# GpSimd's arithmetic moved to VectorE, into copies' scale, and into six merged operations

## The chip, the cores and the metric

The kernel runs on one core of one Trainium2 chip. The metric is the device time of one execution in microseconds (us). A core has five engines with queues of their own: PE (TensorE, matrix products), DVE (VectorE), ACT (ScalarE), POOL (GpSimd) and SP (SyncE, which here only issues DMAs). Each engine works through its queue in order; an instruction that waits holds back all that is queued behind it on the same engine.

## What is computed

Two small transformer stacks run one after the other on 512 tokens of width 1024, in float32. The first has two layers of a mixer (pooling, differential attention and a bidirectional recurrent branch, gated and summed) with a feed-forward part; every sum is followed by a layer norm. The second has two layers with a sparse and a banded attention, whose queries and keys get a root-mean-square norm per head, a weight per head column, and on one branch a partial rotation:

```python
x = layer_norm(alpha * x + mix, ln1_g[l], ln1_b[l])
hid = jnp.square(jax.nn.relu(x @ w_up[l]))
x = layer_norm(alpha * x + hid @ w_down[l], ln2_g[l], ln2_b[l])
...
qa = partial_rope(rms_norm(qa.reshape(b, s_len, 8, 64), qn_a[l]), cos, sin)   # first 16 of 64 columns rotate
ka = partial_rope(rms_norm(ka.reshape(b, s_len, 1, 64), kn_a[l]), cos, sin)[:, :, 0]
qi = partial_rope(qi.reshape(b, s_len, 8, 64), cos, sin)
ki = partial_rope(ki.reshape(b, s_len, 1, 64), cos, sin)[:, :, 0]
qb = rms_norm(qb.reshape(b, s_len, 8, 64), qn_b[l])
kb = rms_norm(kb.reshape(b, s_len, 8, 64), kn_b[l])
```

## The kernel before

**Matrix products.** Every large product is made three times with float32 values split in two parts, high and low (`mm3`, L235 to L237): high by high, high by low, low by high. A weight chunk of 128x1024 arrives by an SP DMA into `wraw` (three buffers), ACT copies it to `whi` (L228, two buffers), and DVE subtracts to get `wlo` (L229, two buffers). PE then spends 24 matmuls on the chunk. So DVE has one subtraction in each chunk that PE must have before the third matmul of the chunk, and the next chunk's DMA needs a `wraw` that this subtraction has let go.

**The iterator beside.** `chunk` calls `next(self.beside, None)` once for each weight chunk; other work (in the feed-forward part of the first stack, the `ada` product of the second stack's modulation, L1274) is spread over chunks in that way. Which instruction goes where in an engine's queue is settled when the program is built, by the framework's estimate of when its inputs are there, not by the order of the source alone.

**The residual.** A layer-normed tile is written to DRAM without its weight and bias, and read back for the residual by `load_x`: two row vectors `lng` and `lnb` broadcast to 128 partitions, four tiles of 128x1024, and for each tile a product (L381) and a sum (L382) on GpSimd. It is called four times: in each layer of the first stack ahead of the `w_out` product (tiles `xr`, wanted by its first evacuation, L1141), and ahead of the feed-forward part (tiles `xo`, wanted by the first evacuation of `w_down`, L973). The place of the first call is the end of the recurrent branch: there DVE works on the last head pair's norm (L927 to L936, with an inverse root made of a dozen operations on 128x8, L304 to L321), PE on the branch product `merge1` (PSUM tile `mr`), and after it DVE merges the branches (`mgg`, L522, L523) for the `w_out` product.

**The second stack's heads.** `projections` makes `qi`, `qa`, `qb`, `kb` (128 x 4 x 512 each) and two small ones, `ki` and `ka`, one after another, with a norm (`head_norm`), a rotation (`rope`) and transposes (`z_split`, `z_T`) between the products. The norm's last step, the product with the head weight `gn`, is on GpSimd (L1323), and so are all 24 operations of a rotation (L1333 to L1335, four times six). The index scores (`ix`, L1447) and the top-k search (MAX8 L1461, MATCH_REPLACE8 L1462) run on DVE in the same stretch.

Of the kernel before, what the change touches and what calls it, by code (L numbers as in the profile page):

```python
# [10 lines left out]
F32 = mybir.dt.float32  # L11
F32R = mybir.dt.float32r
I32 = mybir.dt.int32
AF = mybir.ActivationFunctionType
# [122 lines left out]
def bcast(ap, n=128):  # L137
    return bass.AP(tensor=ap.tensor, offset=ap.offset, ap=[[0, n]] + [list(x) for x in ap.ap])
# [29 lines left out]
class Kern:  # L168
# [206 lines left out]
    def load_x(self, wk, x, xd, rows):  # L375

        nc = self.nc
        g, b = self.ln_rows(wk, rows)
        for tk in range(4):
            nc.sync.dma_start(x[tk], xd[:, tk, :])  # L380
            nc.gpsimd.tensor_tensor(out=x[tk], in0=x[tk], in1=g, op=OP.mult)  # L381
            nc.gpsimd.tensor_tensor(out=x[tk], in0=x[tk], in1=b, op=OP.add)  # L382


    def bias_setup(self, wk, pp):
# [626 lines left out]
    def layer1(self, l, xd, act, start):  # L1012
# [3 lines left out]
        with tc.tile_pool(name="mx", bufs=1) as mx:  # L1016
# [64 lines left out]
            with tc.tile_pool(name="rw", bufs=1) as rw:  # L1081
                wk = _Slots(rw, MERGE_SLOTS)

                def z_tile(p):
                    vv = wk.tile([128, 640], F32, name="rw_v")
                    nc.vector.memset(vv[:, 0:64], 0.0)
                    nc.vector.memset(vv[:, 576:640], 0.0)
                    rkv = (wk.tile([128, S], F32, name="rw_r"), wk.tile([128, S], F32, name="rw_k"), vv)
                    for i in range(3):
                        dst = vv[:, 64:576] if i == 2 else rkv[i]  # L1090
                        self.lin_fm(pp, w_in, 2048 + i * 512 + p * 128, 1, act, 8,
                                    lambda _, ps: self.shift(wk, ps, vec, i * 4 + p, None, dst))
# [12 lines left out]

                gates = self.gate_steps(mx, pp, act, w_in, hbg, pd, md, gd)
                done = [0]

                def fill(n):
                    for _ in range(n):  # L1110
                        next(gates, None)
                    done[0] += n

                fill.upto = lambda n: fill(max(n - done[0], 0))
                mg = []
                merge = self.merge1(wk, pp, yc, a["w_branch"][l, 2], md, gd, mg)

                def behind():
                    list(gates)
                    for p in range(2):  # L1120
                        t = wk.tile([128, S], F32, name="ycr")
                        nc.scalar.dma_start(t, yd[p])
                        yc[p] = yhl(p)
                        self.split(*yc[p], t)
                    next(merge)

                self.rwkv(wk, pp, l, vec, hb, ka, low, z_tile, y_out, fill, behind)
                for p in range(4):
                    self.dump(f"yc{l}{p}", yc[p])
                act = self.xT()  # L1130
                xd1 = self.dr.tile([128, 4, D], F32, name="xspill", bufs=2)
                next(merge)
                xr = [wk.tile([128, D], F32, name="xr") for _ in range(4)]
                self.load_x(wk, xr, xd, (0, 1) if l == 0 else (6, 8))
                cols = self.ln_cols(wk, (2 + l, 4 + l))
                st = self.new_stats(wk)
                for ch in range(2):
                    cs = slice(ch * 512, (ch + 1) * 512)

                    def ev(tk, ps):  # L1140
                        nc.vector.scalar_tensor_tensor(out=xr[tk][:, cs], in0=xr[tk][:, cs], scalar=alpha, in1=ps,  # L1141
                                                       op0=OP.mult, op1=OP.add)
                        self.stats(st[:, tk], xr[tk], ch)
                        if ch == 1:
                            self.norm_tile(wk, pp, xr[tk], st[:, tk], cols, tk, act, xd1, FILL["lag"][1])

                    self.lin_tm(pp, a["w_out"][l], [(ch * 512, (ch + 1) * 512)], mg, 8, ev,
                                own=wk, tail=FILL["tails"][1] if ch else 1)
# [5 lines left out]
            self.second_consts()  # L1154
        with tc.tile_pool(name="f1", bufs=1) as wk:
            xo = wk.tile([128, 4, D], F32, name="xo")
            self.load_x(wk, [xo[:, tk, :] for tk in range(4)], xd1, (2 + l, 4 + l))
            cols = self.ln_cols(wk, (6 + l, 8 + l))
            g2, b2 = self.ln_rows(wk, (6 + l, 8 + l), nc.gpsimd) if last else (None, None)
            st = self.new_stats(wk)  # L1160
# [24 lines left out]
                else:  # L1185
                    self.norm_tile(wk, pp, xo[:, tk, :], st[:, tk], cols, tk, box[0], xd2, FILL["lag"][2])

            self.beside = chain([None] * 6, self.ada(wk, pp, l, "xhat" if last else "araw"))
            self.ffn1(wk, pp, l, act, xo, after)
            list(self.beside)  # L1190
        if last:
# [116 lines left out]
        self.lag(tk, lambda: self.affine_T(wk, pp, xn, tk, k2["g"][:, 8 * i:8 * i + 8],  # L1308
                                           k2["s"][:, 16 * i:16 * i + 8], act, bufs), lag)

    def head_norm(self, wk, z, g, n):

        nc = self.nc
        ss = wk.tile([128, 4, n], F32, name="hss", bufs=2)
        for t in range(4):
# [4 lines left out]
        zz = z.rearrange("p t h d -> p (t h) d")  # L1320
        nc.vector.tensor_tensor(out=zz, in0=zz, in1=ss.rearrange("p t h -> p (t h)")[:, :, None]
                                .to_broadcast([128, 4 * n, 64]), op=OP.mult)
        nc.gpsimd.tensor_tensor(out=zz, in0=zz, in1=g[:, None, :].to_broadcast([128, 4 * n, 64]), op=OP.mult)  # L1323

    def rope(self, wk, z, n):
        nc = self.nc
        t = wk.tile([128, 4, n, 4, 8], F32, name="ropet", bufs=1)
        for tk in range(4):
            c = self.cos[:, tk, None, :].to_broadcast([128, n, 8])
            s = self.sin[:, tk, None, :].to_broadcast([128, n, 8])  # L1330
            x1, x2 = z[:, tk, :, 0:8], z[:, tk, :, 8:16]
            for i, (x, w) in enumerate(((x1, c), (x2, s), (x2, c), (x1, s))):
                nc.gpsimd.tensor_tensor(out=t[:, tk, :, i, :], in0=x, in1=w, op=OP.mult)  # L1333
            nc.gpsimd.tensor_tensor(out=x1, in0=t[:, tk, :, 0, :], in1=t[:, tk, :, 1, :], op=OP.subtract)
            nc.gpsimd.tensor_tensor(out=x2, in0=t[:, tk, :, 2, :], in1=t[:, tk, :, 3, :], op=OP.add)  # L1335

    def z_split(self, pp, z, dst):

        nc = self.nc
        for j in range(4):  # L1340
            ps = pp.tile([128, 4, 128], F32, name="tr")
            for tk in range(4):
                nc.tensor.transpose(ps[:, tk, :], z[:, tk, j * 128:(j + 1) * 128], self.ident)
            self.stack(dst, ps.rearrange("p a b -> p (a b)"), 2 * j)

    def stack(self, dst, ps, j):

        nc = self.nc
        for m, r in enumerate(HALVES):
            nc.scalar.activation(dst[r, j + m, :], ps[r], AF.Copy)  # L1350
        for m, r in enumerate(HALVES):
            nc.vector.tensor_tensor(out=dst[HALVES[1 - m], j + m, :], in0=ps[r], in1=dst[r, j + m, :].bitcast(F32),
                                    op=OP.subtract)

    def z_T(self, pp, z, dst):

        nc = self.nc
        split = isinstance(dst, tuple)
        for j in range(1 if split else 4):
# [4 lines left out]
            if split:  # L1364
                self.split(*dst, flat)
            else:
                nc.scalar.activation(dst[:, j, :], flat, AF.Copy)

    def attend(self, wk, pp, heads, qb, done=None):

# [146 lines left out]
    def projections(self, wk, zp, pp, l, act, zt, after):  # L1517
        nc, a = self.nc, self.a
        w_in = a["w_in_2"][l]
        gn = wk.tile([128, 4, 64], F32, name="gn")  # L1520
        nc.sync.dma_start(gn.rearrange("p a d -> p (a d)"), bcast(a["qkn"][l].rearrange("a d -> (a d)")))
        for j in (0, 2):
            nc.vector.tensor_scalar(gn[:, j, :], gn[:, j, :], 0.125, None, op0=OP.mult)

        def proj(cols, dst):
            w = sum(c1 - c0 for c0, c1 in cols)
# [17 lines left out]
        nc.vector.tensor_copy(zt["va"], sml[:, :, 0:128][:, :, 64:128])  # L1544
        ka = wk.tile([128, 4, 1, 64], F32, name="ka")
        nc.vector.tensor_copy(ka[:, :, 0, :], sml[:, :, 0:64])
        self.head_norm(wk, ka, gn[:, 1, :], 1)
        self.rope(wk, ka, 1)
        dup = []
        for src in (ki, ka):  # L1550
            dd = wk.tile([128, 4, 2, 64], F32, name="dup", bufs=2)
            nc.gpsimd.tensor_copy(dd[:, :, 0, :], src[:, :, 0, :])
            nc.gpsimd.tensor_copy(dd[:, :, 1, :], src[:, :, 0, :])
            dup.append(dd.rearrange("p t a d -> p t (a d)"))
        qi = z()
        proj([(640, 1152)], qi)
# [6 lines left out]
        after()  # L1563
        qk = zp.tile([128, 8, S], F32, name="qkb", tag="qiT")
        zt["qbT"], zt["kbT"] = qk[:, :4], qk[:, 4:]
        self.head_norm(wk, hv(qa, 8), gn[:, 0, :], 8)
        self.rope(wk, hv(qa, 8), 8)
        qb = z()
        proj([(1224, 1736)], qb)
        self.z_split(pp, qa, zt["qaT"])  # L1570
        self.head_norm(wk, hv(qb, 8), gn[:, 2, :], 8)
        kb = z()
        proj([(1736, 2248)], kb)
        self.z_T(pp, qb, zt["qbT"])
        self.head_norm(wk, hv(kb, 8), gn[:, 3, :], 8)
        proj([(2248, 2760)], zt["vb"])
        self.z_T(pp, kb, zt["kbT"])

    def gate_steps2(self, wk, pp, act, w_in, hb, gd):

# [206 lines left out]
```

## Time and profile before

| | |
|---|---|
| median of 3 runs | 3813.1 us (3811.29 to 3816.84) |
| the profiled execution | 3811.36 us |
| its span, first to last instruction | 3809.4 us |
| PE busy | 3653.1 us, 96% of the span |
| DVE busy | 2272.0 us, 60% |
| ACT busy | 1381.6 us, 36% |
| POOL busy | 294.8 us, 8% |
| granted clock of TensorE, mean | 0.986 of full speed |

Busy time of DVE counts an instruction from its start to its end, and so also the time in which it stands still in the middle. A granted clock of 1.00 is 2.4 GHz, of 0.50 is 1.2 GHz.

### The profile page before, as it was taken

Reading aid. Unit: us, or ns where it says so; the run is one execution under the profiler, and the core shown is the slowest. Engines: PE = TensorE matmul, PEld = TensorE weight load, DVE = VectorE, ACT = ScalarE, POOL = GpSimd, SP = SyncE. Lnnn points to the kernel's source line nnn. Section 1 sums busy time; section 2 is a strip of 40 time slices with the busy share of each in tenths; the row PEclk is TensorE's granted clock in tenths of the full one; section 3 lists DMA queues with packets and bytes.
Section 4 is the critical chain, followed back from the end, with each engine's and each line's share of the span. In section 5 each row is a group of like instructions: output and inputs, shape, how many; then the busy total and the mean of one; then the engine's idle time right before and its main releaser. Section 6 shows DMA issues by size and latency. Waiting matters only on the chain. (4 is left out here: it accounts for less than half of the span.)

```text
span 3809.4 us, 54409 instructions
## 1 busy us (share of the span) xinstructions
PE 3653.1 (96%) x21264; PEld 2845.4 (75%) x21264; DVE 2272.0 (60%) x4679; ACT 1381.6 (36%) x2361; POOL 294.8 (8%) x445
## 2 busy tenths in 40 slices
PE   8999997999999999997899989999999999999999
PEld 6677775778877777765788776768888877678887
DVE  5667775765566577757655549866333369664333
ACT  4543332332334443332323234454222343534221
POOL 0000002110000000002300032000000041000000
PEclk9999999999999999998999999999999999999999
DMA  4333332555552333234555532334332323253332
GB/s 147 122 106 94 84 93 99 169 162 183 165 159 83 101 101 84 79 101 134 169 182 172 163 108 67 114 106 158 99 95 98 116 89 89 78 172 121 97 97 94
DMA packets 509392, 452.22 MB, mean 119 GB/s; under 512 B 87984, under 2 KB 405104, under 8 KB 509136
## 3 DMA queue, kind: packets, MB, share of 16 engines
q1 hardware_dynamic: 492032, 400.88, 34.5%
q0 software_dynamic: 10192, 32.15, 2.4%
q10 hardware_dynamic: 6912, 15.73, 1.2%
q8 instruction: 167, 2.74, 0.3%
q14 instruction: 89, 0.73, 0.1%
HBM read 395.68 MB, written 53.01 MB: 118 GB/s over the span
## 5 line engine op out<-in xcount | busy, mean ns | idle before, releaser
L229 DVE TENSOR_TENSOR wlo<-wraw,whi 128x1024 fp32r<-128x1024 f32 (+2 forms) x496 | 624.9, 1260 | 817.2 <-ACT whi L228 802.0
L228 ACT ACTIVATE whi<-wraw 128x1024 fp32r<-128x1024 f32 (+2 forms) x496 | 523.3, 1055 | 1520.6 <-PE acc L236 612.3
L235 PE MATMUL acc<-xTh,whi 128*128 128x512 f32 (+1 forms) x2320 | 917.7, 396 | 4.5 <-ACT whi L228 2.1
L237 PE MATMUL acc<-xTh,wlo 128*128 128x512 f32 (+1 forms) x2320 | 901.8, 389 | 19.1 <-DVE wlo L229 19.1
L236 PE MATMUL acc<-xTl,whi 128*128 128x512 f32 (+1 forms) x2320 | 899.7, 388 | 3.8 <-POOL xTl L359 1.8
L237 PEld LDWEIGHTS acc<-xTh,wlo 128*128 128x128 f32 x2320 | 438.9, 189 | 109.8 <-DVE wlo L229 20.8
L235 PEld LDWEIGHTS acc<-xTh,whi 128*128 128x128 f32 x2320 | 438.3, 189 | 109.8 <-issue 19.4
L236 PEld LDWEIGHTS acc<-xTl,whi 128*128 128x128 f32 x2320 | 439.2, 189 | 88.5 <-issue 5.1
L235 PE MATMUL tm<-whi,hidh 128*128 128x512 f32 x784 | 307.2, 392 | 0.9 <-DVE xo L975 0.8
L236 PE MATMUL tm<-wlo,hidh 128*128 128x512 f32 x784 | 306.5, 391 | 0.0
L237 PE MATMUL tm<-whi,hidl 128*128 128x512 f32 x784 | 306.5, 391 | 0.0
L235 PEld LDWEIGHTS tm<-whi,hidh 128*128 128x128 f32 x784 | 147.2, 188 | 35.6 <-issue 3.2
L235 PE MATMUL tm<-whi,xTh 128*128 128x512 f32 (+1 forms) x448 | 171.0, 382 | 1.6 <-DVE zt L1532 1.6
L237 PEld LDWEIGHTS tm<-whi,hidl 128*128 128x128 f32 x784 | 147.2, 188 | 31.9
L236 PEld LDWEIGHTS tm<-wlo,hidh 128*128 128x128 f32 x784 | 147.2, 188 | 31.8
L237 PE MATMUL tm<-whi,xTl 128*128 128x512 f32 (+1 forms) x448 | 170.6, 381 | 0.0
L236 PE MATMUL tm<-wlo,xTh 128*128 128x512 f32 (+1 forms) x448 | 170.5, 380 | 0.0
L1274 DVE SCALAR_TENSOR_TENSOR asum<-araw,cc,asum 128x768 f32<-128x768 f32 x112 | 113.7, 1015 | 43.3 <-DMA araw<-in_w_ada_dram 42.4
L1694 DVE TENSOR_TENSOR hT<-hT,acc 128x512 f32<-128x512 f32 x44 | 30.2, 687 | 132.4 <-PE acc L237 125.1
L556 DVE CUSTOM_DVE_ANT_0 L<-lg,G 128x512 f32<-128x512 f32 (+3 forms) x128 | 74.0, 586 | 45.3 <-PE lg L1491 23.6
L359 POOL TENSOR_TENSOR xTl<-hT,xTh 128x512 fp32r<-128x512 f32 x32 | 41.1, 1285 | 771.8 <-DVE xTh L358 431.3
L235 PEld LDWEIGHTS tm<-whi,xTh 128*128 128x128 f32 x448 | 85.4, 191 | 19.4 <-issue 5.1
(479 smaller groups left out, 5641.9 us busy)
## 6 DMA issues: line engine op xcount, KB each, us to landing
wraw<-in_w_in_dram SPq DMA_DIRECT2D x182, 512.0 KB, 3.9
wraw<-in_w_down_dram SPq DMA_DIRECT2D x108, 512.0 KB, 3.6
araw<-in_w_ada_dram SPq DMA_DIRECT2D x128, 384.0 KB, 3.9
wraw<-in_w_gu_dram SPq DMA_DIRECT2D x88, 512.0 KB, 3.8
wraw<-in_w_up_dram SPq DMA_DIRECT2D x64, 512.0 KB, 4.2
wraw<-in_w_out_dram SPq DMA_DIRECT2D x32, 512.0 KB, 3.6
wraw<-in_w_branch_dram SPq DMA_DIRECT2D x18, 512.0 KB, 3.5
prd<-gt POOLq DMA_DIRECT2D x32, 256.0 KB, 2.9
```

Of the source, the lines that this page charges most:

```text
L228: nc.scalar.activation(hi[:, :n], raw[:, :n], AF.Copy)
L229: nc.vector.tensor_tensor(out=lo[:, :n], in0=raw[:, :n], in1=hi[:, :n].bitcast(F32), op=OP.subtract)
L235: nc.tensor.matmul(ps, st[0], mv[0], start=start, stop=False)
L236: nc.tensor.matmul(ps, st[0], mv[1], start=False, stop=False)
L237: nc.tensor.matmul(ps, st[1], mv[0], start=False, stop=stop)
L359: (nc.gpsimd if half else nc.vector).tensor_tensor(out=lo, in0=t, in1=hi.bitcast(F32), op=OP.subtract)
L556: nc.vector.tensor_tensor_reduce(L, ps, bias, -1.0, -LOW, OP.add, OP.min, nmx)
L1274: nc.vector.scalar_tensor_tensor(out=acc, in0=w, scalar=cc[:, k:k + 1], in1=acc, op0=OP.mult, op1=OP.add)
L1694: nc.vector.tensor_tensor(out=t[j], in0=t[j], in1=ps, op=OP.mult)
```

## The change

The weight and the bias of the residual become DVE operations, given out one tile for each weight chunk. The head weights of `qb` and `kb` and the unrotated part of `qa` go into the scale of the ACT copies (and the scalar of the DVE subtractions) that evacuate the transposes, from a column tile `gc` that two GpSimd DMAs fill; its first 16 rows of column 0 are set to one, since `qa`'s first 16 columns get their weight ahead of the rotation. A rotation becomes six DVE operations over all four token tiles. The four copies of `dup` go to ACT.

```diff
 def load_x(self, wk, x, xd, rows):
         for tk in range(4):
             nc.sync.dma_start(x[tk], xd[:, tk, :])
-            nc.gpsimd.tensor_tensor(out=x[tk], in0=x[tk], in1=g, op=OP.mult)
-            nc.gpsimd.tensor_tensor(out=x[tk], in0=x[tk], in1=b, op=OP.add)
+        def steps():
+            for tk in range(4):
+                nc.vector.tensor_tensor(out=x[tk], in0=x[tk], in1=g, op=OP.mult)
+                nc.vector.tensor_tensor(out=x[tk], in0=x[tk], in1=b, op=OP.add)
+                yield
+        return steps()
 # layer1, ahead of w_out
-                self.load_x(wk, xr, xd, (0, 1) if l == 0 else (6, 8))
+                weigh = self.load_x(wk, xr, xd, (0, 1) if l == 0 else (6, 8))
+                self.beside = chain([None], weigh)
                     def ev(tk, ps):
+                        for _ in weigh:
+                            pass
 # layer1, feed-forward
-            self.load_x(wk, [xo[:, tk, :] for tk in range(4)], xd1, (2 + l, 4 + l))
+            weigh = self.load_x(wk, [xo[:, tk, :] for tk in range(4)], xd1, (2 + l, 4 + l))
-            self.beside = chain([None] * 6, self.ada(wk, pp, l, "xhat" if last else "araw"))
+            self.beside = chain([None] * 2, weigh, self.ada(wk, pp, l, "xhat" if last else "araw"))
 # head_norm
-        nc.gpsimd.tensor_tensor(out=zz, in0=zz, in1=g[:, None, :].to_broadcast([128, 4 * n, 64]), op=OP.mult)
+        if g is not None:
+            w = g.shape[1]
+            nc.vector.tensor_tensor(out=zz[:, :, :w], in0=zz[:, :, :w],
+                                    in1=g[:, None, :].to_broadcast([128, 4 * n, w]), op=OP.mult)
 # rope: 24 GpSimd operations become
+        for i, (x, w) in enumerate(((x1, c), (x2, s), (x2, c), (x1, s))):
+            nc.vector.tensor_tensor(out=t[:, i], in0=x, in1=w, op=OP.mult)
+        nc.vector.tensor_tensor(out=x1, in0=t[:, 0], in1=t[:, 1], op=OP.subtract)
+        nc.vector.tensor_tensor(out=x2, in0=t[:, 2], in1=t[:, 3], op=OP.add)
 # stack (of z_split); z_T likewise
-            nc.scalar.activation(dst[r, j + m, :], ps[r], AF.Copy)
+            nc.scalar.activation(dst[r, j + m, :], ps[r], AF.Copy, **({} if g is None else {"scale": g[r]}))
+                nc.vector.scalar_tensor_tensor(out=lo, in0=ps[r], scalar=g[r], in1=hi, op0=OP.mult, op1=OP.subtract)
 # projections
+        gc = wk.tile([128, 4], F32, name="gc")
+        for r in HALVES:
+            nc.gpsimd.dma_start(gc[r], a["qkn"][l].rearrange("a d -> d a"))
+            nc.vector.tensor_scalar(gc[:, j:j + 1], gc[:, j:j + 1], 0.125, None, op0=OP.mult)   # j = 0, 2
+            nc.vector.memset(gc[r.start:r.start + 16, 0:1], 1.0)
-            nc.gpsimd.tensor_copy(dd[:, :, 0, :], src[:, :, 0, :])
-            nc.gpsimd.tensor_copy(dd[:, :, 1, :], src[:, :, 0, :])
+                nc.scalar.activation(dd[:, :, i, :], src[:, :, 0, :], AF.Copy)
-        self.head_norm(wk, hv(qa, 8), gn[:, 0, :], 8)
+        self.head_norm(wk, hv(qa, 8), 8, gn[:, 0, :16])
-        self.head_norm(wk, hv(qb, 8), gn[:, 2, :], 8)
-        self.head_norm(wk, hv(kb, 8), gn[:, 3, :], 8)
+        self.head_norm(wk, hv(qb, 8), 8)
+        self.head_norm(wk, hv(kb, 8), 8)
```

## Rows read from the trace of the kernel before

**Rows 1.** The page, part 1: busy time, share and instructions of each engine.

```profile
PE 3653.1 (96%) x21264; PEld 2845.4 (75%) x21264; DVE 2272.0 (60%) x4679; ACT 1381.6 (36%) x2361; POOL 294.8 (8%) x445
```

**Rows 2.** Stretches: start:end, length, busy (count): PE, PEld, DVE, ACT, POOL; clock; DMA share; GB/s.

```profile
632.00:652.40 20.40, 5.39 (x23) 3.73 (x21) 20.17 (x9) 2.38 (x3) 18.99 (x9) 0.73 0.18 72
652.40:658.20 5.80, 5.80 (x14) 4.54 (x15) 1.49 (x3) 0.00 (x0) 0.00 (x0) 0.50 0.49 158
764.90:772.60 7.70, 0.16 (x2) 0.01 (x1) 7.67 (x4) 1.68 (x3) 7.54 (x4) 0.68 0.30 81
772.60:778.00 5.40, 5.40 (x13) 4.24 (x14) 5.40 (x5) 0.00 (x0) 2.16 (x1) 0.51 0.33 88
1728.60:1744.10 15.50, 0.03 (x1) 0.00 (x0) 15.16 (x14) 0.45 (x1) 12.29 (x6) 0.66 0.00 0
1744.10:1750.00 5.90, 5.89 (x21) 4.79 (x22) 1.08 (x1) 0.64 (x1) 0.00 (x0) 0.73 0.54 178
1852.40:1859.80 7.40, 0.10 (x2) 0.10 (x1) 7.37 (x4) 1.53 (x3) 7.24 (x4) 0.78 0.31 89
1859.80:1865.20 5.40, 5.40 (x17) 4.33 (x18) 5.40 (x5) 0.00 (x0) 3.14 (x3) 0.67 0.46 156
2355.00:2371.00 16.00, 11.30 (x49) 8.91 (x49) 15.90 (x34) 5.61 (x9) 3.81 (x1) 0.89 0.22 66
3160.00:3175.00 15.00, 11.20 (x39) 8.40 (x38) 14.91 (x40) 5.60 (x9) 1.71 (x1) 0.66 0.24 70
```

**Rows 3.** What PE waited for, whole span: total us, times, longest.

```profile
PE mr L237 <- DVE wlo L229: 30.4, 2, 15.5
PE acc L237 <- DVE wlo L229: 19.1, 5, 7.5
...
PE sc L1419 <- ACT rl L1442: 3.8, 2, 1.9
```

**Rows 4.** Timeline of DVE and POOL at the `xr` tiles: start, length, instruction.

```profile
631.62 0.17 DVE L319 TENSOR_TENSOR rqt<-rqy 128x8 f32<-128x8 f32 x1
641.30 9.75 DVE L319 TENSOR_TENSOR rqt<-rqy 128x8 f32<-128x8 f32 x1
...
646.38 4.63 POOL L382 TENSOR_TENSOR xr<-xr,lnb 128x1024 f32<-128x1024 f32 x2
...
1724.32 14.24 DVE L310 TENSOR_SCALAR rqy<-rqy 128x8 int32<-128x8 int32 x1
```

**Rows 5.** Timeline of POOL and DVE at a head weight of the second stack.

```profile
2354.23 4.57 POOL L1323 TENSOR_TENSOR zt<-zt,gn 128x2048 f32<-128x2048 f32 x1 [21.30 <-DVE zt L1321]
...
2354.32 5.58 DVE L229 TENSOR_TENSOR wlo<-wraw,whi 128x1024 fp32r<-128x1024 f32 x1
...
2315.37 4.92 DVE L1447 SCALAR_TENSOR_TENSOR ix<-rl,wi,ix 128x384 f32<-128x384 f32 x1 [0.24 <-ACT rl L1442]
```

**Rows 6.** Durations: one line's forms (ns min/median/max); one group (busy us, mean ns).

```profile
L229 DVE TENSOR_TENSOR wlo<-wraw,whi x496: 783/1225/5575, 20.0 to 3784.4; 128x1024 fp32r<-128x1024 f32 x161, 128x768 fp32r<-128x768 f32 x3, 128x600 fp32r<-128x600 f32 x2
...
L1321 DVE TENSOR_TENSOR ka<-ka,hss 128x256 f32<-128x256 f32 x1 | 0.4, 424 | 0.0
```

**Rows 7.** POOL's product groups of the residual: busy us, mean ns, idle before, releasers.

```profile
L381 POOL TENSOR_TENSOR xo<-xo,lng 128x1024 f32<-128x1024 f32 x8 | 20.0, 2504 | 18.0 <-DMA xo<-xspill 18.0
...
L381 POOL TENSOR_TENSOR xr<-xr,lng 128x1024 f32<-128x1024 f32 x8 | 18.8, 2368 | 12.9 <-DMA lng<-in_ln_dram 8.9 <-issue 4.0
```

**Rows 8.** Timelines at the second stack's start; a column-wise POOL DMA and its landing.

```profile
2223.23 0.30 DVE L1523 TENSOR_SCALAR gn<-gn 128x64 f32<-128x64 f32 x2 [4.43 <-DMA gn<-in_qkn_dram]
2223.44 1.22 DVE L229 TENSOR_TENSOR wlo<-wraw,whi 128x1024 fp32r<-128x1024 f32 x1
...
2224.87 0.39 PE L237 MATMUL tm<-xTh,wlo 128*128 128x512 f32 x1
...
L1506 POOL DMA_DIRECT2D mc<-mod x8: 896/932/938, 1685.2 to 2143.2; - x8
DMA to landing us min/median/max: 2.9/4.5/5.5
```

More of the change, by code (lines that the diff above doesn't have):

```diff
@@ L1309, in rms_tile, with head_norm @@
                                            k2["s"][:, 16 * i:16 * i + 8], act, bufs), lag)
-    def head_norm(self, wk, z, g, n):
+    def head_norm(self, wk, z, n, g=None):
         nc = self.nc
@@ L1322, in head_norm, with z_split @@
                                 .to_broadcast([128, 4 * n, 64]), op=OP.mult)
-        nc.gpsimd.tensor_tensor(out=zz, in0=zz, in1=g[:, None, :].to_broadcast([128, 4 * n, 64]), op=OP.mult)
+        if g is not None:
+            w = g.shape[1]
+            nc.vector.tensor_tensor(out=zz[:, :, :w], in0=zz[:, :, :w],
+                                    in1=g[:, None, :].to_broadcast([128, 4 * n, w]), op=OP.mult)
     def rope(self, wk, z, n):
         nc = self.nc
[L1327 to L1337, printed above, removed]
+        t = wk.tile([128, 4, 4, n, 8], F32, name="ropet", bufs=1)
+        c, s = (w[:, :, None, :].to_broadcast([128, 4, n, 8]) for w in (self.cos, self.sin))
+        x1, x2 = z[:, :, :, 0:8], z[:, :, :, 8:16]
+        for i, (x, w) in enumerate(((x1, c), (x2, s), (x2, c), (x1, s))):
+            nc.vector.tensor_tensor(out=t[:, i], in0=x, in1=w, op=OP.mult)
+        nc.vector.tensor_tensor(out=x1, in0=t[:, 0], in1=t[:, 1], op=OP.subtract)
+        nc.vector.tensor_tensor(out=x2, in0=t[:, 2], in1=t[:, 3], op=OP.add)
+    def z_split(self, pp, z, dst, g=None):
         nc = self.nc
@@ L1343, in z_split, with stack, z_T @@
                 nc.tensor.transpose(ps[:, tk, :], z[:, tk, j * 128:(j + 1) * 128], self.ident)
-            self.stack(dst, ps.rearrange("p a b -> p (a b)"), 2 * j)
-    def stack(self, dst, ps, j):
+            self.stack(dst, ps.rearrange("p a b -> p (a b)"), 2 * j, g)
+    def stack(self, dst, ps, j, g=None):
         nc = self.nc
         for m, r in enumerate(HALVES):
-            nc.scalar.activation(dst[r, j + m, :], ps[r], AF.Copy)
+            nc.scalar.activation(dst[r, j + m, :], ps[r], AF.Copy, **({} if g is None else {"scale": g[r]}))
         for m, r in enumerate(HALVES):
-            nc.vector.tensor_tensor(out=dst[HALVES[1 - m], j + m, :], in0=ps[r], in1=dst[r, j + m, :].bitcast(F32),
-                                    op=OP.subtract)
-    def z_T(self, pp, z, dst):
+            lo, hi = dst[HALVES[1 - m], j + m, :], dst[r, j + m, :].bitcast(F32)
+            if g is None:
+                nc.vector.tensor_tensor(out=lo, in0=ps[r], in1=hi, op=OP.subtract)
+            else:
+                nc.vector.scalar_tensor_tensor(out=lo, in0=ps[r], scalar=g[r], in1=hi, op0=OP.mult, op1=OP.subtract)
+    def z_T(self, pp, z, dst, g=None):
         nc = self.nc
@@ L1366, in z_T @@
             else:
-                nc.scalar.activation(dst[:, j, :], flat, AF.Copy)
+                nc.scalar.activation(dst[:, j, :], flat, AF.Copy, scale=g)
     def attend(self, wk, pp, heads, qb, done=None):
@@ L1521, in projections @@
         nc.sync.dma_start(gn.rearrange("p a d -> p (a d)"), bcast(a["qkn"][l].rearrange("a d -> (a d)")))
+        gc = wk.tile([128, 4], F32, name="gc")
+        for r in HALVES:
+            nc.gpsimd.dma_start(gc[r], a["qkn"][l].rearrange("a d -> d a"))
         for j in (0, 2):
             nc.vector.tensor_scalar(gn[:, j, :], gn[:, j, :], 0.125, None, op0=OP.mult)
+            nc.vector.tensor_scalar(gc[:, j:j + 1], gc[:, j:j + 1], 0.125, None, op0=OP.mult)
+        for r in HALVES:
+            nc.vector.memset(gc[r.start:r.start + 16, 0:1], 1.0)
         def proj(cols, dst):
@@ L1546, in projections @@
         nc.vector.tensor_copy(ka[:, :, 0, :], sml[:, :, 0:64])
-        self.head_norm(wk, ka, gn[:, 1, :], 1)
+        self.head_norm(wk, ka, 1, gn[:, 1, :])
         self.rope(wk, ka, 1)
@@ L1551, in projections @@
             dd = wk.tile([128, 4, 2, 64], F32, name="dup", bufs=2)
-            nc.gpsimd.tensor_copy(dd[:, :, 0, :], src[:, :, 0, :])
-            nc.gpsimd.tensor_copy(dd[:, :, 1, :], src[:, :, 0, :])
+            for i in range(2):
+                nc.scalar.activation(dd[:, :, i, :], src[:, :, 0, :], AF.Copy)
             dup.append(dd.rearrange("p t a d -> p t (a d)"))
@@ L1569, in projections @@
         proj([(1224, 1736)], qb)
-        self.z_split(pp, qa, zt["qaT"])
-        self.head_norm(wk, hv(qb, 8), gn[:, 2, :], 8)
+        self.z_split(pp, qa, zt["qaT"], gc[:, 0:1])
+        self.head_norm(wk, hv(qb, 8), 8)
         kb = z()
         proj([(1736, 2248)], kb)
-        self.z_T(pp, qb, zt["qbT"])
-        self.head_norm(wk, hv(kb, 8), gn[:, 3, :], 8)
+        self.z_T(pp, qb, zt["qbT"], gc[:, 2:3])
+        self.head_norm(wk, hv(kb, 8), 8)
         proj([(2248, 2760)], zt["vb"])
-        self.z_T(pp, kb, zt["kbT"])
+        self.z_T(pp, kb, zt["kbT"], gc[:, 3:4])
     def gate_steps2(self, wk, pp, act, w_in, hb, gd):
```

## The prediction, made before the change was run

> **What bounds the kernel now.** I read the page's first part first [rows 1]: PE is busy 3653.1 of 3809.4 us, so it is the engine that sets the end, and POOL, from which the change takes work, is busy only 8%. Freeing POOL itself can therefore give nothing. At most the 156.3 us that PE is idle, and the time in which it runs at the lower of its two clock levels, can come back. So I read next what PE waits for, over the whole span [rows 3]. The longest single waits are two of 15 us for a DVE subtraction, `wlo`, in the `merge1` product, and two of 7.5 us for the same thing in another product: 30.4 us in 2 and 19.1 us in 5. A subtraction takes 1.225 us at the median but 5.575 at worst [rows 6], so something holds DVE back. The third view is the stretches around these waits [rows 2], the fourth the timeline of DVE and POOL in them [rows 4].
>
> There the reader sees the mechanism on which I rest. A DVE product on 128x8 takes 0.17 us at 631.62, and 9.75 us, the same line and shape, at 641.30. It ends at 651.05, within 0.04 us of POOL's last sum on `xr` (646.38 + 4.63 = 651.01). In the other layer a 128x8 DVE operation takes 14.24 us. DVE is recorded as busy (20.17 of 20.40 us), but with nine instructions: it stands still while POOL's arithmetic runs. The subtraction for PE is queued behind them, PE does 5.39 us of work in 20.40, and afterwards runs 5.80 us at a granted clock of 0.50, the 1.2 GHz level [rows 2]. The second stack shows it in small: POOL's head weight runs from 2354.23 to 2358.80 and a `wlo` started at 2354.32 takes 5.58 us, ending 1.1 us after it [rows 5].
>
> **What the change gives back.** A stretch's loss is its length less PE's busy time, and in the stretch behind it busy time times the missing share of the clock [rows 2].
> - `xr`, two layers: 15.01 + 5.80 × 0.50 = 17.9, and 15.47 + 5.89 × 0.27 = 17.1. Sum 35.0 us.
> - `xo`, two layers: 7.54 + 5.40 × 0.49 = 10.2, and 7.30 + 5.40 × 0.33 = 9.1. Sum 19.3.
> - Heads and rotation: in 2355 to 2371 4.70 + 11.30 × 0.11 = 5.9; in 3160 to 3175 3.80 + 11.20 × 0.34 = 7.6; and the two waits of 1.9 for ACT's `rl` [rows 3], which stood behind an index score of 4.92 us [rows 5]: 3.8. Sum 17.3.
>
> Gross 71.6 us. Three further `acc` waits, 19.1 − 7.54 − 7.30 = 4.3 us with perhaps 1.5 of clock behind them, I leave out of the sum and put into the lower end.
>
> **What it adds, and where that lies.** Each residual step is two DVE operations on 128x1024; the same size costs 1.225 us as a subtraction [rows 6]. Four calls of eight: 39.2 us. In each second-stack layer there are two rotations of eight heads, six operations of 128x256 at 0.424 [rows 6], 5.1 us; the weight of `qa`'s rotated columns, 128x512, between 0.42 and 1.225, say 0.7; `ka`'s weight 0.42; and two small rotations of twelve operations between 0.17 [rows 4] and 0.42, near the lower, say 2.2. That is 8.4 a layer, 16.8 in all. So 56 us come to an engine at 60%, 1381.6 of 3809.4 on ACT makes the four `dup` copies and the scales free there, and almost all DVE work lies beside PE. Where the cover is missing:
> - **`xr`'s steps near the root.** The iterator hands them out behind the first chunk of `w_out`, but the order in DVE's queue is settled by an estimate, so some may stand among the root's small operations or ahead of the merge of the branches, on which `w_out` waits. Bounds 0, and all sixteen of both layers in the path, 16 × 1.225 = 19.6. I take 4, some three of the sixteen: nearer the lower end, since PE has whole chunks to do between the first hand-out and the first evacuation, which is where the tiles are wanted.
> - **`xo`'s steps and their DMA.** POOL waited 18.0 us in all for the DMA that brings `xo` back from DRAM, and for `xr` 12.9 us, 8.9 of it for `lng` [rows 7]. Now DVE would wait, and the `wlo` of the next chunks behind it, and PE behind that. A chunk is 24 matmuls; 14 of them took 5.80 us at half clock [rows 2], so 0.21 each at full and 5.0 us a chunk. With two chunks ahead of the steps most of the data has landed. Bounds 0 and 18.0 for `xo`; I take 1.
> - **`gc`.** Two column-wise DMAs go onto POOL's queue at the start of each second-stack layer, and two scalings and two `memset`s of theirs onto DVE. There DVE already waits 4.43 us for `gn`, with a `wlo` right behind at 2223.44 (1.22), and PE uses it at 2224.87: 0.2 us of slack [rows 8]. A column-wise POOL DMA takes 0.93 us to issue and lands 2.9 to 5.5 later, two in a row then 1.86 + 2.9 to 1.86 + 5.5 after the first begins. If the first begins as that wait does, it lengthens by up to 7.4 − 4.4 = 3 and half a microsecond of small operations; bounds 0 and 3.5 a layer. I take 3 for both layers.
> - **Second stack.** DVE is busy 15.90 of 16.00 us there [rows 2]. Of the 17.3, bounds 0 and 17.3, I take 4 as not returned, since the added 16.8 us stand in this same stretch, while the standstill they replace cost DVE more: 4.36 us extra in one `wlo` alone [rows 5, 6].
>
> Back 4 + 1 + 3 + 4 = 12, net 71.6 − 12 = 59.6. The profiled execution takes 3811.36 us (its span 3809.4, 2.0 around it), the median is 3813.1, 1.7 higher. 3811.4 − 59.6 = 3751.8, on the median 3753.5: forecast **3753**. With nothing given back 3741.5; with the three further waits too, 3735.7. The forecast's own range is 3736 to 3770.
>
> **The rivals.**
> - **DVE inherits POOL's waits for DMA.** All 12.9 + 18.0 = 30.9 us [rows 7] come to stand ahead of a `wlo`. For: DVE's queue is in order, and `wlo` is in it every chunk. Against: the steps are put behind one and two chunks. Back 12 − 1 + 30.9 = 41.9, net 29.7: 3813.1 − 29.7 = 3783.
> - **DVE saturated in the second stack.** It gains nothing there and the added 16.8 us lengthen it: back 4 + 1 + 3 + 17.3 + 16.8 = 42.1, net 29.5: 3784. For: 15.90 of 16.00. Against: part of that busy time is the standstill itself (5.58 instead of 1.225). The Trainium skill ("Perfetto Trace Analysis", "Optimizing Scalar/DVE Operations") says that with DVE saturated, work may be moved off it, even to GPSIMD, though the shared port can undo that; by the first half the change goes the wrong way here and the time would be this rival's 3784, by the second it is the forecast's 3753, and the 5.58 us row bears out the second.
> - **Slower: the added DVE time all falls ahead of a subtraction that PE waits for.** The place is the chunk: PE's third matmul of each needs `wlo`, and weights ahead of it in DVE's queue delay it. The price is 39.2 + 16.8 + 30.9 = 86.9 us against 71.6 gained: 3813.1 + 15.3 = 3828. It decides once more than 71.6 of the 86.9, four fifths, is exposed. Against: two steps and a subtraction, 3 × 1.225 = 3.7 us, fit in a chunk's 5.0 us, and two `wlo` buffers let DVE run a chunk ahead.
> - **No change: DVE's long rows are not POOL's doing.** Then only work changes place: 3813. Against: the end within 0.04 us of POOL's, and PE's stretches end with it in four places.
>
> **How the numbers follow.** Forecast 0.74; DMA waits 0.10; saturated 0.06; slower 0.05; no change 0.05. The first three are faster by over 0.2% (7.6 us, about what a measurement of this kernel tells from no change): 0.90; same 0.05; slower 0.05. The range 3735 to 3784 takes in both bounds of the terms and the first two rivals, and leaves out about 0.15.
>
> **What would show it.** Right: the 30.4 us wait of `mr` for `wlo` is gone [rows 3], PE's clock stays 1.00 behind the `merge1` product, the longest `wlo` falls from 5575 ns to about 1.3 us, POOL has no arithmetic in these stretches, and the index scores of 4.92 us are short. Partly wrong: DVE rows with idle before them released by the DMA of `xo`, `lng` or `gc`, with PE waiting behind; a new PE wait for `wlo` at the start of the second stack's layers; PE waits for `mgg` that grow (the weights stood ahead of the merge). Wrong: 128x8 DVE rows of microseconds with POOL silent, which would mean that the lock was something else.

## The result, and the profile after

The changed kernel takes 3763.4 us (median of four runs, 3757.6 to 3765.0) against 3813.9 for the kernel before: a ratio of 0.9865, with a 95% interval of 0.9848 to 0.9882. That is 50.5 us, where 60 were forecast. The profiled execution took 3762.69 us, its span 3760.9.

First the page's busy line of the changed kernel, and what PE waited for over the whole span (total us, times, longest).

```profile
PE 3641.2 (97%) x21264; PEld 2836.8 (75%) x21264; DVE 2233.0 (59%) x4771; ACT 1386.4 (37%) x2369; POOL 121.7 (3%) x209
```

```profile
PE tm L236 <- DVE wlo L229: 16.0, 7, 6.1
...
PE ll L945 <- DVE ytm L942: 7.7, 4, 3.8
...
PE tm L235 <- DVE mgg L528: 7.5, 4, 2.6
PE acc L237 <- DVE wlo L229: 4.5, 4, 2.2
```

The 30.4 us of `mr` [rows 3] are gone, and the 19.1 us of `acc` are 4.5. DVE took over some 56 us of arithmetic and is still busy 39 us less than before (2233.0 against 2272.0 [rows 1]): what it lost was time recorded as busy in which it stood still. The other signs that I named came too: in the first layer PE runs at a granted clock of 1.00 behind the start of `merge1`, as the first row below shows (length, busy us and count of PE, PEld, DVE, ACT, POOL, then the clock), and the longest index score is 0.75 us. In the second layer the clock falls further on, for a new wait told below. The worst `wlo` has fallen; the second row has all its durations (ns, min/median/max). The one of 2086 stands in the first chunks, at 22.8 us, beside a GpSimd operation that the change leaves alone; every other is 1.23 us or less.

```profile
631.00:648.00 17.00, 15.78 (x68) 12.17 (x66) 15.34 (x30) 5.01 (x7) 0.54 (x1) 1.00 0.55 194
...
L229 DVE TENSOR_TENSOR wlo<-wraw,whi x496: 782/1225/2086, 19.8 to 3735.8; 128x1024 fp32r<-128x1024 f32 x161, 128x768 fp32r<-128x768 f32 x3, 128x600 fp32r<-128x600 f32 x2
```

Where in the kernel the time came from can be read from the same PE instructions in both traces. These are rows of one line's groups of matmuls, with the start of the first and of the last; the first fence is the kernel before, the second the changed one.

```profile
L237 PE MATMUL tm<-whi,hidl x784: 387/389/398, 835.8 to 3793.7; 128*128 128x512 f32 x196
...
L237 PE MATMUL tm<-xTh,wlo x96: 278/283/415, 2209.3 to 3038.0; 128*128 128x256 f32 x64, 128*128 128x512 f32 x32
```

```profile
L237 PE MATMUL tm<-whi,hidl x784: 388/389/397, 812.1 to 3745.2; 128*128 128x512 f32 x196
...
L237 PE MATMUL tm<-xTh,wlo x96: 278/283/504, 2160.0 to 2989.7; 128*128 128x256 f32 x64, 128*128 128x512 f32 x32
```

At the first `w_down` product the changed kernel is 835.8 − 812.1 = 23.7 us ahead, at the first product of the second stack 2209.3 − 2160.0 = 49.3, at the second stack's second layer 48.3, at the last of the `w_down` products 3793.7 − 3745.2 = 48.5. **The first stack gave everything, and the second gave nothing**, although GpSimd's head weights and rotations are gone from it. When I compare starts below, it is in this way, one matched PE instruction against the other.

Three new waits stand in place of the old ones. The first is in the second stack: in each of its two layers PE waits 6.1 us for a `wlo`. These are rows of the changed kernel's timeline, of DVE, ACT and PE (start, length, instruction, idle time before it):

```profile
2285.29 1.06 ACT L228 ACTIVATE whi<-wraw 128x1024 fp32r<-128x1024 f32 x1 [0.57 <-PE tm L237]
...
2286.97 1.28 DVE L1327 TENSOR_REDUCE hss<-hsq 128x8 f32<-128x512 f32 x2
2288.29 3.04 DVE L1367 SCALAR_TENSOR_TENSOR qaT<-tr,gc,qaT 64x512 fp32r<-64x512 f32 x4
2291.36 1.28 DVE L1327 TENSOR_REDUCE hss<-hsq 128x8 f32<-128x512 f32 x2
2292.56 1.22 DVE L229 TENSOR_TENSOR wlo<-wraw,whi 128x1024 fp32r<-128x1024 f32 x1
...
2293.83 0.80 PE L236 MATMUL tm<-wlo,xTh 128*128 128x512 f32 x1 [6.11 <-DVE wlo L229]
```

Its input `whi` was there at 2286.35, and DVE was never idle: the subtraction stands in DVE's queue behind four reductions and the evacuations of `qa`'s transposes. In the kernel before, the corresponding `wlo` came ahead of them:

```profile
2335.84 1.22 DVE L229 TENSOR_TENSOR wlo<-wraw,whi 128x1024 fp32r<-128x1024 f32 x1
2337.09 2.81 DVE L1352 TENSOR_TENSOR qaT<-tr,qaT 64x512 fp32r<-64x512 f32 x4
```

The second new wait is at the end of the recurrent branch, 3.75 us for `ytm` in the first stack's second layer and 1.2 us in its first. Weights of `xr` stand between the small operations of the root, here in the second layer:

```profile
1700.69 0.16 DVE L309 TENSOR_SCALAR rqy<-rqv 128x8 int32<-128x8 int32 x1
1700.76 1.22 DVE L385 TENSOR_TENSOR xr<-xr,lnb 128x1024 f32<-128x1024 f32 x1
1701.90 0.16 DVE L310 TENSOR_SCALAR rqy<-rqy 128x8 int32<-128x8 int32 x1
1701.97 1.22 DVE L384 TENSOR_TENSOR xr<-xr,lng 128x1024 f32<-128x1024 f32 x1
...
1710.61 0.63 PE L945 MATMUL ll<-cpack,ytm 128*128 128x128 f32 x4 [3.75 <-DVE ytm L942]
```

The third is at `xo`, where the iterator hands out one tile a chunk but DVE's queue has three tiles between two `wlo`:

```profile
1800.43 1.23 DVE L384 TENSOR_TENSOR xo<-xo,lng 128x1024 f32<-128x1024 f32 x1 [1.31 <-DMA xo<-xspill]
...
1802.17 1.22 DVE L385 TENSOR_TENSOR xo<-xo,lnb 128x1024 f32<-128x1024 f32 x1
1803.31 2.35 DVE L384 TENSOR_TENSOR xo<-xo,lng 128x1024 f32<-128x1024 f32 x2
...
1805.91 1.22 DVE L385 TENSOR_TENSOR xo<-xo,lnb 128x1024 f32<-128x1024 f32 x1
...
1807.65 1.22 DVE L385 TENSOR_TENSOR xo<-xo,lnb 128x1024 f32<-128x1024 f32 x1
1808.78 1.22 DVE L229 TENSOR_TENSOR wlo<-wraw,whi 128x1024 fp32r<-128x1024 f32 x1
...
1810.06 0.50 PE L237 MATMUL acc<-xTh,wlo 128*128 128x512 f32 x1 [2.16 <-DVE wlo L229]
```

The shorter wait for `xo`, 1.45 us in the first layer, leaves PE at a granted clock of 1.00; those of 2.16 us for `xo`, 6.11 us for `qa`'s evacuations and 3.75 us for `ytm` (0.64 from 1710.6 to 1720.0) have a lower one in or behind them, as the old stalls had behind them [rows 2]. The rows are those of the first layer's `xo`, the second layer's `xo`, and `qa`, in the form of the `merge1` row above:

```profile
741.00:750.00 9.00, 7.55 (x33) 5.91 (x32) 9.00 (x11) 2.38 (x4) 0.00 (x0) 1.00 0.70 209
...
1804.00:1814.00 10.00, 7.84 (x28) 5.96 (x27) 10.00 (x12) 2.40 (x5) 1.11 (x2) 0.83 0.74 221
2287.00:2299.00 12.00, 5.80 (x17) 4.48 (x18) 11.89 (x33) 3.25 (x6) 0.00 (x0) 0.72 0.38 108
```

### The profile page after: what moved, and what is told of

Read it like the earlier page. It is cut to its first block, busy times and chain, and to the rows that moved or that the text cites. A ratio compares the mean times of both kernels' runs of the same rounds, so it can differ in the third digit from the quotient of the medians.

```text
span 3760.9 us, 54232 instructions
## 1 busy us (share of the span) xinstructions
PE 3641.2 (97%) x21264; PEld 2836.8 (75%) x21264; DVE 2233.0 (59%) x4771; ACT 1386.4 (37%) x2369; POOL 121.7 (3%) x209
## 5 line engine op out<-in xcount | busy, mean ns | idle before, releaser
L229 DVE TENSOR_TENSOR wlo<-wraw,whi 128x1024 fp32r<-128x1024 f32 (+2 forms) x496 | 604.1, 1218 | 786.3 <-ACT whi L228 769.3
L236 PEld LDWEIGHTS tm<-wlo,xTh 128*128 128x128 f32 x448 | 85.6, 191 | 31.5 <-DVE wlo L229 15.0
```

Of the source, the lines that this page charges most:

```text
L229: nc.vector.tensor_tensor(out=lo[:, :n], in0=raw[:, :n], in1=hi[:, :n].bitcast(F32), op=OP.subtract)
L236: nc.tensor.matmul(ps, st[0], mv[1], start=False, stop=False)
```

## The experiments

**One part at a time.** The first-stack part alone takes the hunks of `load_x`, `xr` and `xo`; the second-stack part alone takes the others and leaves the residual where it was:

```diff
 def load_x(self, wk, x, xd, rows):
             nc.sync.dma_start(x[tk], xd[:, tk, :])
+            nc.gpsimd.tensor_tensor(out=x[tk], in0=x[tk], in1=g, op=OP.mult)
+            nc.gpsimd.tensor_tensor(out=x[tk], in0=x[tk], in1=b, op=OP.add)
...
-            self.beside = chain([None] * 2, weigh, self.ada(wk, pp, l, "xhat" if last else "araw"))
+            self.beside = chain([None] * 6, self.ada(wk, pp, l, "xhat" if last else "araw"))
```

> The kernel before with the first-stack part of the change alone: residual weights on DVE, heads and rotation stay on GpSimd. Theory (the whole gain is in the first stack; the second stack's part is worth nothing net): matching PE instructions of before and after, the first stack ends 49.6 us earlier, so 3813.9 - 49.6 = 3764, within 4 us of the whole change. Rival (the second-stack part gives the 13.3 us net of my forecast and the first stack only 46.3 - 13 or so): 3778 or later, well behind the whole change.

> The second-stack part alone: head weights in the scale of copies and rotations on DVE, residual weights stay on GpSimd as before. Theory (its gains are eaten by a wlo that now stands behind the evacuations of qa's transposes): 3814, within 4 us; the two 6 us waits of the second stack's tm L236 for wlo are there, the 1.9 us waits for rl are gone. Rival (forecast): 3813.9 - 10 = 3804.

Measured: the first part 3770.5 us, 0.9893 of before (0.9876 to 0.9909); the second 3812.3, 1.0000 (0.9990 to 1.0009). The second had its 6.1 us waits. The first came out 7 us later than the whole change had been on another occasion, more than the theory wanted, so both were timed once more on one chip.

> The first-stack part alone, timed once more beside the whole change on one chip: their difference is what the second-stack part is worth. Theory (by matched instructions the second stack of the changed kernel gains 0.4 us net and gives back 1.7 at its start): the two within 4 us. Rival (the forecast's 10 us): the whole change is 10 us shorter.

> The whole change, beside the first-stack part alone: 3763, and 0 to 4 us from it by the theory, 10 us shorter by the forecast.

Measured: 3765.7 (0.9866, 0.9853 to 0.9880) and 3765.2 (0.9868, 0.9854 to 0.9881). They are the same, and the second-stack part is worth nothing as it stands. Medians of one kernel on different occasions differ by up to 5 us, so small gains below are read together with their waits.

**What holds DVE up.** GpSimd keeps its eight operations a call on the residual, on the same tiles and of the same length, but with one tensor operand:

```diff
-            nc.gpsimd.tensor_tensor(out=x[tk], in0=x[tk], in1=g, op=OP.mult)
-            nc.gpsimd.tensor_tensor(out=x[tk], in0=x[tk], in1=b, op=OP.add)
+            nc.gpsimd.tensor_scalar(x[tk], x[tk], 2.0, None, op0=OP.mult)
+            nc.gpsimd.tensor_scalar(x[tk], x[tk], 0.5, None, op0=OP.mult)
```

> The kernel before, with GpSimd's eight operations per call on the residual kept at their place and length, but with one tensor operand (times 2, then times 0.5) in the place of two. It leaves out the weights and biases of the residual. Theory (DVE stands still because GpSimd reads two tensors at once): DVE's 128x8 rows are 0.17 us again, PE's two 15 us waits for wlo vanish, and the time is that of the first-stack part, 3764, or a little below, since DVE has less to do. Rival (any arithmetic of GpSimd of that length makes DVE stand still): the 15 us waits stay, 3814.

Measured: 3760.6 us, 0.9867 (0.9852 to 0.9881), and the 15 us waits are gone. At `xr` GpSimd starts at other times than before, since it no longer waits for `lng`; the clean comparison is `xo`, where eight operations run in a row in both. The timeline there, first of the kernel before, then of this one:

```profile
756.41 2.62 DVE L964 CAST hidh<-relu 128x512 fp32r<-128x512 f32 x1
...
761.76 2.36 DVE L1262 TENSOR_SCALAR cct<-cct 128x8 f32<-128x8 f32 x1
764.15 2.29 DVE L1263 TENSOR_TENSOR cc<-cc,cct 128x8 f32<-128x8 f32 x1
...
769.18 3.36 DVE L229 TENSOR_TENSOR wlo<-wraw,whi 128x1024 fp32r<-128x1024 f32 x1
```

```profile
742.59 2.81 POOL L381 TENSOR_SCALAR xo<-xo 128x1024 f32<-128x1024 f32 x1
...
743.01 0.64 DVE L1262 TENSOR_SCALAR cct<-cct 128x8 f32<-128x8 f32 x1 [1.12 <-ACT cct L1261]
743.68 0.17 DVE L1263 TENSOR_TENSOR cc<-cc,cct 128x8 f32<-128x8 f32 x1
...
744.42 1.22 DVE L229 TENSOR_TENSOR wlo<-wraw,whi 128x1024 fp32r<-128x1024 f32 x1
745.56 1.26 DVE L964 CAST hidh<-relu 128x512 fp32r<-128x512 f32 x1
```

GpSimd is busy for longer than before (2.8 us an operation against 2.5), and yet PE's stalls are gone. But DVE is not left alone. The `wlo` above started 1.8 us after its GpSimd operation; one that starts together with a GpSimd operation is held up, as these rows of the same kernel show:

```profile
1625.94 2.77 POOL L381 TENSOR_SCALAR xr<-xr 128x1024 f32<-128x1024 f32 x1 [8.55 <-DMA xr<-xspill]
1625.97 2.09 DVE L229 TENSOR_TENSOR wlo<-wraw,whi 128x1024 fp32r<-128x1024 f32 x1
```

It takes 0.87 us more than the usual 1.22, the cast above 0.83 more than its usual 0.43, and a 128x8 row that starts with a GpSimd operation at 1702.97 takes 1.02 us, where the theory had 0.17; the next one, still within that operation, takes 0.17. In the kernel before, the four rows shown are held 2.1 to 2.2 us each, nearly a whole GpSimd operation, and the next operation catches the next row. So a GpSimd operation with one operand holds DVE too, some 0.85 us of its 2.8, where one with two holds it 2.1 of 2.5. The edit changes the kind of the instruction together with its operands (`tensor_scalar` for `tensor_tensor`), so that it is the second tensor is not shown by itself. Where this kernel's GpSimd still reads two, in the second stack, a `wlo` still stands still:

```profile
2306.81 4.58 POOL L1323 TENSOR_TENSOR zt<-zt,gn 128x2048 f32<-128x2048 f32 x1 [21.36 <-DVE zt L1321]
...
2306.89 5.57 DVE L229 TENSOR_TENSOR wlo<-wraw,whi 128x1024 fp32r<-128x1024 f32 x1
```

The Trainium skill ("SBUF — State Buffer", "Who interferes with whom") says that a DVE instruction with two SBUF inputs contends with a GpSimd instruction that reads SBUF. The `wlo` at 1625.97, which has two inputs, agrees: it was held though GpSimd read one tensor only.

**The three new waits, one by one.** `issue_after` queues what it encloses behind a given instruction on that instruction's engine, without a wait. `self.wlo` is the latest chunk's subtraction when a step is handed out.

```diff
 def chunk(...):
-        nc.vector.tensor_tensor(out=lo[:, :n], ...)
+        self.wlo = nc.vector.tensor_tensor(out=lo[:, :n], ...)
 def load_x(...):      # paced: for xr in one kernel, for xo in the other
+                with self.tc.issue_after(self.wlo.ins) if paced else ExitStack():
                     nc.vector.tensor_tensor(out=x[tk], in0=x[tk], in1=g, op=OP.mult)
                     nc.vector.tensor_tensor(out=x[tk], in0=x[tk], in1=b, op=OP.add)
 # layer1, feed-forward: in the kernel for xo
-            self.beside = chain([None] * 2, weigh, self.ada(...))
+            self.beside = chain([None] * 5, weigh, self.ada(...))
```

> The whole change, with each of xr's weight steps queued on DVE behind the wlo of the chunk before it, so that none stands among the operations of the root. Theory (in the second layer the root ends late because seven steps stand between its operations; PE waits 3.75 us for ytm): that wait falls to about 1.4 us as in the layer before or below, and 3 to 5 us are gained on the changed kernel: about 3759. Rival (the root is late for another reason, or the steps now delay mgg by as much): 3763, and PE's wait for mgg grows by what ytm's shrinks.

> The whole change, with xo's weight steps started three chunks later, each queued on DVE behind the wlo of the chunk before it: one tile between two wlo. Theory (PE's waits of 1.5 and 2.2 us for wlo there come from three tiles standing between two wlo, 7.2 us of DVE work in a chunk of about 5.4): both waits vanish with the lower clock behind them, 1.8 + 4.1 = 5.9 us: about 3757. Rival (DVE waits for the DMA of xo, 0.59 and 1.31 us, and that is what delays wlo): waits of DVE for xo vanish too, but the gain is at most those 1.9 us: 3761.

Measured: `xr` 3760.3 us (0.9865, 0.9850 to 0.9880), `xo` 3756.4 (0.9854, 0.9840 to 0.9869): 3.1 and 7.0 us under the changed kernel's 3763.4. With `xr`'s steps out of the way the root ends in one piece:

```profile
1700.42 0.17 DVE L320 TENSOR_TENSOR rqt<-rqt,rqv 128x8 f32<-128x8 f32 x1
1700.62 0.17 DVE L321 SCALAR_TENSOR_TENSOR gvar<-rqt,rqy 128x8 f32<-128x8 f32 x1
1700.82 0.76 DVE L943 TENSOR_TENSOR ytm<-ytm,gvar 128x256 f32<-128x256 f32 x2
```

`ytm` is started at 1700.82, 2.42 us after the root's first operation at 1698.40; in the changed kernel it took from 1698.61 to 1709.70, 11.1 us. The rival came in part: the steps now stand ahead of a `wlo` of the same layer's `w_out` product, where PE waits for it.

```profile
1730.06 0.50 PE L236 MATMUL tm<-wlo,mgh 128*128 128x512 f32 x1 [3.06 <-DVE wlo L229]
```

By matched PE instructions the second layer's root came 5.6 us earlier and its `w_out` lost 1.5 of that; in the first layer it was 1.2 and 0.4. The gain of 3.1 us alone is no more than these medians can carry; with the rows it stands.

For `xo`, neither PE's waits for `wlo` nor DVE's for `xo` are left, and matched PE instructions gained 1.6 us in the first layer and 4.1 in the second. That is 5.7 us, as the theory had it, where the DMA waits explain at most 1.9; the medians' 7.0 could not tell the two apart. But the later start takes away the DMA waits together with the crowding, so how PE's 3.6 us of waiting divide between them is not shown.

The third kernel hands out `qa`'s transposes one at a time over the chunks of `kb`'s product:

```diff
-        self.z_split(pp, qa, zt["qaT"], gc[:, 0:1])
+        steps = self.z_steps(pp, qa, zt["qaT"], gc[:, 0:1], True)   # z_split as a generator, each stack behind self.wlo
         self.head_norm(wk, hv(qb, 8), 8)
         kb = z()
+        self.beside = chain([None], steps)
         proj([(1736, 2248)], kb)
+        list(steps)
```

> The whole change, with the transposes of qa and their evacuations handed out one at a time over the chunks of kb's product, each evacuation queued on DVE behind the wlo of the chunk before. DVE's work is the same. Theory (the second stack's gain was lost because one wlo per layer stands behind eight evacuations and four reductions in DVE's queue): PE's two waits of 6.1 us go, with 2 us of lower clock behind each, 14 to 16 us in all: about 3748. Rival (DVE is saturated there, so whatever is moved makes another wlo late): 3760 to 3764.

Measured: 3750.3 us, 0.9840 (0.9825 to 0.9855), 13.0 under the changed kernel. PE's waits in this stretch of the first layer, where the 6.1 us stood:

```profile
PE tm L235 <- DVE zt L1555: 2.6, 1, 2.6
PE tm L236 <- DVE wlo L229: 0.9, 1, 0.9
PE tr L1379 <- ACT qkb L1384: 0.4, 1, 0.4
```

DVE does the same operations, so the rival, saturation, falls. By matched instructions the two layers gained 6.4 and 8.0 us; the 2.6 us for an evacuation (`zt`) is what is late next. The same order with the second-stack part alone:

> The kernel before with the second-stack part and the new order of qa's evacuations, the residual on GpSimd as before. Theory (the second-stack part is worth its gross 17.3 us once no wlo stands behind the evacuations, less 1.7 for gn and gc): 3813 - 15 = 3798. Rival (the order is worth something only with the first stack's part, or the gain of 13 us was chance): 3806 or later.

Measured: 3799.5 us against 3816.1 for the kernel before on that chip, 16.6 us, 0.9958 (0.9944 to 0.9971, so some 11 to 21 us). The part of the change that was worth nothing is worth that with one `wlo` a layer put ahead. By matched PE instructions of the profiled executions the second stack gained 12.3.

**All three orders together.**

> The whole change with all three new orders (xr's steps, xo's steps, qa's evacuations). Theory: the three gains add, 4 + 5.9 + 15 = 25 us on the changed kernel: about 3739, which is the forecast's gross gain and the bonus of stalls on araw that vanished. Rival (the waits hide one another): about 3748.

Measured: 3738.6 us, 0.9808 (0.9792 to 0.9825), the fastest of all, 24.8 under the changed kernel. The single gains, 3.1 + 7.0 + 13.0 = 23.1, add.

**An attempt at the wait for `gn` and `gc`.** The loads and scalings move into a pool that is open from the first stack's end:

```diff
 def second_consts(self):
         self.k2p = self.ctx.enter_context(self.tc.tile_pool(name="k2", bufs=1))
+        self.head_w = [self.head_weights(l) for l in range(2)]
 def projections(...):
-        gn = wk.tile([128, 4, 64], F32, name="gn")
...
+        gn, gc = self.head_w[l]
```

> All three new orders, and gn and gc loaded and scaled in the feed-forward part of the first stack's last layer, for both layers, in place of at each second-stack layer's start. Theory (DVE's wait for gn and gc delays one wlo per layer, which cost 1.7 us in the changed kernel): 2 us less than with the three orders, 3737. Rival (the wlo is late for another reason): 3739, the same.

Measured: 3753.2 us, 0.9837 (0.9823 to 0.9850). Neither answer: 14.6 us slower. Against the kernel with the three orders, matched PE instructions gained 1.0 us at the start of the second stack's second layer and nothing at the first's, so the wait was worth at most half of what was expected. And in long stretches of `w_down`, with PE at full clock and without a wait, it lost some 0.7 us in every 25. The next kernel only shifts tiles:

```diff
         self.k2p = self.ctx.enter_context(self.tc.tile_pool(name="k2", bufs=1))
+        for l in range(2):
+            for n, w in (("gn", 128), ("gc", 4)):
+                self.nc.vector.memset(self.k2p.tile([128, w], F32, name=f"{n}{l}"), 0.0)
```

> The three new orders, with gn and gc loaded where they were, but four small tiles (128 and 4 columns, twice) set to zero and otherwise unused at the place where the kernel with early loads keeps gn and gc. They shift the addresses of later tiles by the same amount. Theory (in the kernel with early loads the products of w_down ran at 396 ns a matmul and not 389 for long stretches, and took 13 us more, because its tiles lie elsewhere in SBUF): the same stretches are slow, 3751 to 3755. Rival (the early loads or the changed order of DVE make them slow): 3739.

Measured: 3751.7 us, 0.9841 (0.9823 to 0.9860). The empty tiles alone cost 13 us. A group of matmuls from 3645 to 3695 us, first of the kernel with the three orders, then of this one (busy us, mean ns):

```profile
L235 PE MATMUL tm<-whi,hidh 128*128 128x512 f32 x74 | 28.8, 389 | 0.0
```

```profile
L235 PE MATMUL tm<-whi,hidh 128*128 128x512 f32 x72 | 28.5, 396 | 0.0
```

The same matmul takes 7 ns longer by its record, and fewer of them fit; PE is busy through the whole stretch in both. The first layer's `w_down` product, near 870 us, is at 396 ns in both, as in the kernels before and after the change; only the three later products differ.

## Why the prediction was right, point by point

The direction, the mechanism and the range held; the forecast's 60 us were 50.5. Matched PE instructions give each term.

- **`xr` 35.0, `xo` 19.3.** The stalls gave back 17.9 + 17.1 = 35.0 and 10.3 + 9.2 = 19.5. That the 128x8 rows stood still for GpSimd, read from two ends 0.04 us apart [rows 4], is borne out by the kernel with one operand, in which the two stalls of 15 us are gone. That PE's stretches end with GpSimd's work in four places holds for the two `xr` only. At `xo` PE goes on at 772.60, with GpSimd busy for 2.16 us more [rows 2]: DVE gets about one instruction in for each GpSimd operation, and the wait ends when the `wlo` has had its turn.
- **Steps near the root, 4.** Measured 5.0 behind the two stalls, 3.6 in the second layer and 1.4 in the first. In size right, and there for the reason named: they stand among the root's operations. Queued behind the chunk's `wlo`, they let the root end 5.6 and 1.2 us earlier, and 1.5 and 0.4 of that went again in `w_out`.
- **`xo`'s steps, 1.** Measured 5.9 (1.8 and 4.1). This step failed. I costed the DMA that DVE would wait for, and that was nearly right: 1.9 us of idle DVE. The rest is work that stands between two `wlo`, as far as the two can be told apart. I took it that a generator which hands out a tile a chunk puts a tile between two `wlo`. My bound for it, two steps and a subtraction within a chunk, was the bound of an order that the queue does not have. The steps became ready late, after the iterator had handed out three, and then stood together.
- **`gc`, 3.** The two layers' starts lost 0.6 and 1.1 us, 1.7 in all. PE waited 0.27 us behind the scalings of `gc` in the first and 0.86 in the second, where DVE waited 0.66 us for the DMA of `gc`.
- **Second stack, 17.3 less 4.** This is the step that was most wrong. By matched instructions the new waits and the loads of `gc` took 8.2 + 7.6 + 1.7 = 17.5 us, and the second stack ended 0.8 us worse than nothing (49.3 down to 48.5), so some 16.7 must have come. The gross term was about right, as far as the 11 to 21 us of the second-stack part in the other order can show it. What took it back was neither of the two reasons that I had weighed, added DVE work and saturation. With the rotation earlier done, `qa`'s transposes were placed earlier and their eight evacuations came ahead of the next `wlo`: 6.1 us of idle PE in each layer and some 2 at the lower clock behind it. The prediction asked what was late next only for operations that the change adds; this one was merely moved.
- **Left out.** In the first stack's second layer a further stall behind the `xo` one disappeared too, for 5.3 us. It is the longest of the three `acc` waits, 3.4 of 4.3 us, that I kept out of the sum and in the lower end. In the kernel before, the `wlo` stood behind an `ada` step (`asum`) that waited for its DMA:

```profile
1873.75 1.02 DVE L1274 SCALAR_TENSOR_TENSOR asum<-araw,cc,asum 128x768 f32<-128x768 f32 x1 [2.57 <-DMA araw<-in_w_ada_dram]
...
1874.69 1.22 DVE L229 TENSOR_TENSOR wlo<-wraw,whi 128x1024 fp32r<-128x1024 f32 x1
...
1875.96 0.50 PE L237 MATMUL acc<-xTh,wlo 128*128 128x512 f32 x1 [3.40 <-DVE wlo L229]
```

  It went with the `xo` stall in the kernel with one operand as well (4.9 us) and stayed, at 2.3 us, with the second-stack part alone, which keeps that stall. So it goes with that stall, though its size is not steady; why the DMA is in time without the stall was not tested. Other differences of 1.5 us and under, of both signs, make up the rest.

So 35.0 + 19.5 + 5.3 − 5.0 − 5.9 − 1.7 = 47.2, next to 48.5 in the spans, with the second stack at nothing. That the 50.5 come so near the 60 is in part luck: without the 5.3 us, which I had not counted, it would be 45.

Of the rivals, the DMA waits came to little (1.9 us of idle DVE for `xo`, 1.3 for `lng`, of 30.9), and the saturated second stack gave the right result there, nothing gained, for the wrong reason. The Trainium skill ("Perfetto Trace Analysis", "Optimizing Scalar/DVE Operations") says that work may be moved off a saturated DVE, with the reservation that moving it to GpSimd might not help, for the port that the two share. Here moving it the other way, with part of it going into ACT's scale and fewer operations, gained the 16.6 us once the order was right, so the measurement goes with the reservation.

## What to carry to other kernels

A busy engine can be one that stands still: compare one operation's duration in a quiet stretch with its worst, and look for what ends at the same time. When work is moved to the engine that also feeds the bottleneck, what counts is which operations stand between two of those that the bottleneck waits for, so read that queue's order, also for operations that the change only lets start earlier. Handing work out in small portions does not space it unless the order is stated, and one such order, that of `qa`'s evacuations, was worth 13 us of the 25 to be had.

## What the runs showed of the hardware

- A DVE instruction that starts with a GpSimd operation on 128x1024 stands still, and the time is recorded as busy: by 0.8 to 0.9 us when GpSimd runs `tensor_scalar` on one tensor for 2.8 us (`wlo` 2.09 us against 1.22), by 2.1 to 2.2 when it runs `tensor_tensor` on two for 2.5 (`wlo` 3.36, a 128x8 product 2.29 against 0.17). One that started 1.8 us after the one-tensor operation was not held.
- How long a matmul takes depends on where tiles lie: with PE at its full clock and no wait, 389 ns became 396 in the same product when four small unused tiles shifted the rest. Over the kernel that was 13 us, half of what the three orders gained. Which address matters was not tried.
